# Up weights prepared ahead of the second half's output weights, odd blocks loaded whole, first transposes one block later

## The chip, the core and the metric

The kernel runs on one core of one Trainium2 chip. The metric is device time in microseconds (us), the median of three runs; of one further run there is a hardware profile of every engine. Engines are named as the profile names them: PE is the matrix engine, PEld its weight loads, DVE the vector engine, ACT the scalar engine, POOL is GpSimd, and SP issues the DMAs that are spoken of here.

## The reference, cut to what matters

One hybrid decoder layer over 1024 tokens and 16 meta tokens ahead of them, width 1024:

```python
a = rmsnorm(h, ln_mix_pre[l])
proj = a @ w_in[l]
...
y_diff = diff_attention(dq, dk, dv, ...)
y_hgrn = hgrn2(hq, hf, hi, hg, ...)
mix = jnp.concatenate([y_diff, y_hgrn], axis=-1) @ w_out[l]
h = h + rmsnorm(mix, ln_mix_post[l])
a = rmsnorm(h, ln_ffn_pre[l])
y = conv_ffn(a, w_ffn_up[l], ...)
h = h + rmsnorm(y, ln_ffn_post[l])
```

The change lies where the mixer output is multiplied with `w_out`, normalized, and turned into the transposed input of the up projection.

## The kernel before

**Precision.** Every float32 operand of a product is split into a high and a low part (`split`: an ACT cast makes the high part, a subtraction on DVE or POOL the low one). A product is then three matmuls: high by high, high by low, low by high. `out_part` issues these three for each 128 rows k of `w_out` (L943, L945, L947).

**The stage.** Tokens stand in nine blocks: block 0 is two meta tokens, blocks 1 to 8 are 128 tokens each. `w_out` is used in two halves of 512 output columns. `out_first` does the first half while the last HGRN head (`hgrn_head`) is still being computed: `mix_split` makes high and low parts of the mixer output, hands them to PE in tiles `mm` (four buffers) and stores them to DRAM (`msc`, L932). The k = 7 part depends on the last head and comes last (`out_last`, tiles `pz`). The loop behind it does the second half in the order of blocks 1, 0, 2, 3 ... 8: four pieces c of two k each, read from tiles `mp` that `mix_load` (L950, DMA at L955) brings back from `msc`. There are four `mp` tiles, so piece c of the next block is loaded when PE has read piece c of this one. After a block, `post` loads the residual `xh` (two buffers), normalizes, stores `hsc`, squares on ACT, and makes `a2` on DVE. `trans` (L1061; PE transposes at L1068, ACT copies into `at2`) turns an `a2` round; it stands in the middle of a block's matmuls, ahead of piece 2: `trans(1)` in block 2, `trans(0)` in block 3, `trans(i-2)` in block i. After blocks 1, 2 and 3 two `out_last` each finish the first half of blocks 3 to 8.

**Weights.** `load_wo(n)` (L902) loads eight raw tiles `wor` of `w_out` (tag "wr", three buffers) and splits each into `woh` and `wol` (nine buffers; the second half's k = 3 and later take the slots that the first half's k = 2 and later leave at the end of `out_first`). Odd k are subtracted on DVE, even k on POOL. The up weights are prepared by `prep_plain` (four raw tiles `ra`, split into `uh` and `ul`) and by `prep(q)`, whose sums `ws` (POOL, L1119) also take a "wr" buffer. `ra` has five buffers.

**Order.** PE runs in the order in which the program is written. The orders of ACT, DVE, POOL and SP are made by a scheduler from data dependences, buffers and the order of the program; each engine then works strictly in its own row. All ACT and DVE operations pass through one helper and carry L53. Mixer groups `mix0`, `mix1`, `mix2` are large tiles that are used up one after the other as blocks are split; used-up ones are reused for later tiles.

Of the kernel before, what the change touches and what calls it, by code (L numbers as in the profile page):

```python
# [85 lines left out]
def layer_kernel(ctx: ExitStack, tc: tile.TileContext, x, meta, table, lbl, gpre, gpost, win,  # L86
# [892 lines left out]
    def out_first():  # L979
# [3 lines left out]
        for n, (i, c) in enumerate(todo):  # L983
            if n + 3 < len(todo):
# [12 lines left out]
            if i == NBLK - 1:  # L997
                mix_load(1, c, 0, 2 if c < 3 else 1)
# [11 lines left out]
    close(ma_cm)  # L1010
    wo = load_wo(1)
    close(h_cm, at_p_cm)
# [9 lines left out]
    at2.reverse()  # L1022
    q_cm, qp = pool("p2", 2, "right")
    gpo = qp.tile([P, 512], F32, tag="gpo", name="gpo", bufs=1)
    SY.dma_start(gpo, gpost[:, 512:].to_broadcast([P, 512]))
# [50 lines left out]

    raws, sums, made = {}, {}, {}

    tt = [[None] * 8 for _ in range(2)]
# [29 lines left out]

    def load_raw4(ft):  # L1110
        raws.clear()
        for nm, m, c in (("11", ft, 0), ("22", ft + NF, 1), ("21", ft + NF, 0), ("12", ft, 1)):
            raws[nm] = swp.tile([P, 512], F32, tag="ra", name=f"ra{ft}_{nm}", bufs=5)
            with tc.issue_after(wo0_loaded.ins):
                SY.dma_start(raws[nm], wup[m][:, 512 * c: 512 * (c + 1)])

    def w_sum(nm, a, b, op):
        sums[nm] = wp.tile([P, 512], F32, tag="wr", name=f"ws{nm}", bufs=3)
        G.tensor_tensor(sums[nm], a, b, op=op)  # L1119
        return sums[nm]  # L1120

    def prep(q):
        ft, j = divmod(q, 7)
        if ft >= NF:
            return
        if j == 0:
            load_raw4(ft)
            src = raws["11"]
            w_sum("1", raws["21"], raws["22"], ALU.add)
        elif j == 1:  # L1130
            src = w_sum("2", sums["1"], raws["11"], ALU.subtract)
        elif j == 2:
            src = sums["1"]
        elif j == 3:
            src = w_sum("3", raws["11"], raws["21"], ALU.subtract)
        elif j == 4:
            src = raws["12"]
        elif j == 5:
            src = raws["22"]
        else:  # L1140
            src = w_sum("4", raws["12"], sums["2"], ALU.subtract)
        where = swp if q % 2 else wp
        hi = where.tile([P, 512], F32R, tag="wh", name=f"uh{q}", bufs=4)
        lo = where.tile([P, 512], F32R, tag="wl", name=f"ul{q}", bufs=4)
        split(hi, lo, src, G if j % 2 == 0 and j else V)
        made[q] = (hi, lo)

    plain = {}

    def prep_plain():  # L1150
        load_raw4(0)
        for j, nm in enumerate(("11", "12", "21", "22")):
            where = swp if j % 2 else wp
            hi = where.tile([P, 512], F32R, tag="wh", name=f"uh{nm}", bufs=4)
            lo = where.tile([P, 512], F32R, tag="wl", name=f"ul{nm}", bufs=4)
            split(hi, lo, raws[nm], G)
            plain[nm] = (hi, lo)
# [404 lines left out]
```

## Time and profile before

| quantity | value |
|---|---|
| runs | 1353.58, 1353.48, 1352.76 us; median 1353.48 |
| the profiled execution's own time | 1350.36 us |
| its span, first to last instruction | 1348.6 us |
| mean granted PE clock | 0.995 |
| PE waits of 480 to 800 us | 5.7 + 5.1 + 3.4 + 2.0 + smaller ones |
| DMA share of 640 to 660 us | 0.87 |

A timeline row gives start and duration in us, engine, line, operation, output and inputs by the program's names, shape, and in brackets the idle time ahead of it and what ended it. Consecutive like instructions stand in one row with a count. Matmul starts are exact and their ends modelled, so the distance between starts is the time of one. In a windows row the numbers are the stretch, its length, the busy time of PE, PEld, DVE, ACT and POOL with counts, the granted clock, the DMA share and GB/s. The view of one tile lists its groups as shortest, median and longest duration in ns, with the first and last start.

### The profile page before, as it was taken

The page shows a single profiled execution, that of the slowest core. Times are in us where ns is not written, and L with a number is a line of the kernel's source. Part 1 is how long each engine was busy: PE and PEld are TensorE (multiplying, and loading weights), DVE is VectorE, ACT ScalarE, POOL GpSimd, SP SyncE. Part 2 cuts the span into 40 slices and gives each one's busy share as a digit, 9 for nine tenths or more (in the row PEclk, how much of TensorE's full clock was granted, in tenths as well). Part 3 has the DMA queues.
Part 4 walks back from the last instruction along what each step waited for, and adds up shares of the span by engine and source line. Part 5 has one row for each costly group of instructions (what it writes and reads, how often), then busy time and mean ns, then how long its engine had stood idle before and what let it go on. Part 6 is the DMA issues. An engine that isn't in the chain of part 4 may idle for free.

```text
span 1348.6 us, 26297 instructions
## 1 busy us (share of the span) xinstructions
PE 1293.3 (96%) x10170; PEld 1188.5 (88%) x10170; DVE 929.0 (69%) x1609; ACT 689.9 (51%) x1641; POOL 422.0 (31%) x334
## 2 busy tenths in 40 slices
PE   6999999999999999998898999999999999999997
PEld 5898999989999998676798999999999998888875
DVE  7565657574747474756798787787787776697586
ACT  7465346534654565455574444454444444554453
POOL 3211211021112110234036656656657640010121
PEclk9999999999999999999999999999999999999999
DMA  6331333133211012747712222223221225964253
GB/s 213 107 132 52 103 125 103 44 127 102 103 52 43 22 48 83 232 143 237 243 43 86 95 78 80 79 85 105 79 87 71 79 82 187 336 198 166 87 203 118
DMA packets 84356, 157.01 MB, mean 116 GB/s; under 512 B 9811, under 2 KB 18547, under 8 KB 84230
## 3 DMA queue, kind: packets, MB, share of 16 engines
q1 hardware_dynamic: 84230, 155.33, 34.3%
q8 instruction: 80, 1.31, 0.4%
q14 instruction: 46, 0.38, 0.1%
HBM read 114.66 MB, written 40.63 MB: 115 GB/s over the span
## 4 chain that ended last, share of the span: by engine, by line
PE 59%; DVE 6%; ACT 4%; DMA 4%; issue 3%; POOL 2%; SPq 0%; DVEq 0%; POOLq 0%; ACTq 0%
PE pd L1408 5%; PE pd L1409 5%; PE pd L1407 5%; PE pb L1249 4%; PE pb L1251 4%; PE pb L1250 4%; PE pc L1249 3%; PE pc L1251 2%; PE pc L1250 2%; PE pa L1249 2%; PE pa L1250 2%; PE pa L1251 2%; PE pa L694 1%; PE py L943 1%; PE py L947 1%
## 5 line engine op out<-in xcount | busy, mean ns | idle before, releaser
L1249 PE MATMUL pb<-t,uh 128*128 128x258 f32 x504 | 143.3, 284 | 5.7 <-DVE u L53 5.7
L1251 PE MATMUL pb<-t,ul 128*128 128x258 f32 x504 | 141.7, 281 | 0.0
L1250 PE MATMUL pb<-t,uh 128*128 128x258 f32 x504 | 141.6, 281 | 0.0
L1408 PE MATMUL pd<-wl,gh 128*128 128x512 f32 x308 | 121.9, 396 | 0.1
L1407 PE MATMUL pd<-wh,gh 128*128 128x512 f32 x308 | 121.7, 395 | 0.0
L1409 PE MATMUL pd<-wh,gl 128*128 128x512 f32 x308 | 121.7, 395 | 0.0
L53 DVE SCALAR_TENSOR_TENSOR c<-uu,cwt,c 128x514 f32<-128x514 f32 (+1 forms) x88 | 96.4, 1096 | 20.6 <-ACT c L53 19.9
L1216 POOL TENSOR_TENSOR c<-c,c 128x514 f32<-128x514 f32 (+1 forms) x44 | 63.4, 1440 | 122.8 <-ACT c L53 118.7
L1249 PEld LDWEIGHTS pb<-t,uh 128*128 128x128 f32 x504 | 94.9, 188 | 7.5 <-DVE u L53 6.9
L1251 PEld LDWEIGHTS pb<-t,ul 128*128 128x128 f32 x504 | 95.2, 189 | 0.0
L1250 PEld LDWEIGHTS pb<-t,uh 128*128 128x128 f32 x504 | 95.2, 189 | 0.0
L1250 PE MATMUL pc<-t,uh 128*128 128x258 f32 (+1 forms) x336 | 95.2, 283 | 0.0
L1249 PE MATMUL pc<-t,uh 128*128 128x258 f32 (+1 forms) x336 | 95.0, 283 | 0.0
L1251 PE MATMUL pc<-t,ul 128*128 128x258 f32 (+1 forms) x336 | 95.0, 283 | 0.0
L1249 PE MATMUL pa<-t,uh 128*128 128x258 f32 (+1 forms) x336 | 94.8, 282 | 0.0
L1250 PE MATMUL pa<-t,uh 128*128 128x258 f32 (+1 forms) x336 | 94.5, 281 | 0.0
L1251 PE MATMUL pa<-t,ul 128*128 128x258 f32 (+1 forms) x336 | 94.2, 280 | 0.0
L53 DVE SCALAR_TENSOR_TENSOR c<-ug,cwt,c 128x514 f32<-128x514 f32 (+1 forms) x88 | 86.1, 978 | 2.7 <-ACT c L53 2.0
L145 POOL TENSOR_TENSOR ul<-ws,uh 128x512 fp32r<-128x512 f32 x42 | 59.5, 1416 | 43.8 <-ACT uh L53 39.3
L1408 PEld LDWEIGHTS pd<-wl,gh 128*128 128x128 f32 x308 | 57.7, 187 | 15.1 <-DVE wl L53 0.9
L1409 PEld LDWEIGHTS pd<-wh,gl 128*128 128x128 f32 x308 | 57.7, 187 | 14.0
L1407 PEld LDWEIGHTS pd<-wh,gh 128*128 128x128 f32 x308 | 57.7, 187 | 14.0
(357 smaller groups left out, 4149.5 us busy)
## 6 DMA issues: line engine op xcount, KB each, us to landing
ra<-in_wup_dram SPq DMA_DIRECT2D x88, 256.0 KB, 2.7
wd<-in_wdown_dram SPq DMA_DIRECT2D x44, 256.0 KB, 4.8
tsc<-wd SPq DMA_DIRECT2D x44, 256.0 KB, 3.1
wi<-tsc SPq DMA_DIRECT2D x44, 256.0 KB, 2.8
gi<-gsc SPq DMA_DIRECT2D x33, 256.0 KB, 4.1
wi<-in_wdown_dram SPq DMA_DIRECT2D x33, 256.0 KB, 2.9
mp<-msc SPq DMA_DIRECT2D x31, 256.0 KB, 4.0
msc<-mm SPq DMA_DIRECT2D x24, 256.0 KB, 2.3
```

Source lines behind the costliest of these rows:

```text
L53: ins = call(*args, **kw)
L145: (eng or G).tensor_tensor(lo, raw, hi.bitcast(F32), op=ALU.subtract)
L694: T.matmul(po[:, :P], w_, vn[:, j], start=(j == 0), stop=(j == i))
L943: T.matmul(py[:r], mh, hi, start=(first and k == k0), stop=False)
L947: T.matmul(py[:r], ml, hi, start=False, stop=(last and k == k1 - 1))
L1216: G.tensor_tensor(cg, cg, cu, op=ALU.mult)
L1249: T.matmul(pt, hi[:, s], th[:, k], start=(first and k == 0), stop=False, skip_group_check=True)
L1250: T.matmul(pt, hi[:, s], tl[:, k], start=False, stop=False, skip_group_check=True)
L1251: T.matmul(pt, lo[:, s], th[:, k], start=False, stop=(k == 3), skip_group_check=True)
L1407: T.matmul(py, gh[:, s], wh, start=(k == 0 and pr not in (3, 7)), stop=False, skip_group_check=True)
L1408: T.matmul(py, gh[:, s], wl, start=False, stop=False, skip_group_check=True)
L1409: T.matmul(py, gl[:, s], wh, start=False, stop=(k == NH - 1), skip_group_check=True)
```

## The change

Three things. First, `prep_plain()` and `prep(7)` (with the nine loads of raw up weights) stand ahead of `load_wo(1)`; before, `prep_plain` stood in the last block and `prep(7)` later still. Second, blocks 3, 5 and 7 get one tile for all four pieces, placed in used-up mixer groups; block 3 is loaded after block 1, block 5 after block 3, block 7 after block 5, and even blocks two blocks ahead into the four `mp` tiles. Third, `trans(1)` moves from block 2 to block 3, directly ahead of `trans(0)`; its `a2` goes to a tile of its own.

```diff
     def mix_load(i, c, k0=0, k1=2):
-        if k0 == 0:
+        if i > 1 and i % 2:
+            if c == 0:
+                loaded[i] = mxp.tile([P, 4, 2, 2, P], F32R, tag=f"mix{i // 4}", name=f"mp{i}")
+            loaded[i, c] = loaded[i][:, c]
+        elif k0 == 0:
             loaded[i, c] = mlp.tile([P, 2, 2, P], F32R, tag="mp", name=f"mp{i}_{c}", bufs=4)
...
-    sps = [pair(1, 0), pair(2, 0), pair(1, 1)]
+    sps = [pair(1, 0), pair(2, 0), pair(1, 1), pair(2, 1)]
...
-    wo = load_wo(1)
     close(h_cm, at_p_cm)
...
+    prep_plain()
+    prep(7)
+    wo = load_wo(1)
     gpo = qp.tile([P, 512], F32, tag="gpo", name="gpo", bufs=1)
...
-        if i >= 3 and i % 2:
+        if i == 1:
+            a2 = ep.tile([P, 8, WN[0]], F32, tag="e0", name="a2_1").rearrange("p a c -> p (a c)")[:, :D]
+        elif i >= 3 and i % 2:
...
-        if i == NBLK - 1:
-            prep_plain()
...
-                if i >= 2:
-                    trans((1, 0, 2, 3, 4, 5, 6)[i - 2])
+                if i == 3:
+                    trans(1)
+                    trans(0)
+                if i > 3:
+                    trans(i - 2)
...
-            if i + 1 < NBLK:
-                mix_load(i + 1, c)
+            if i == 1:
+                mix_load(2, c)
+            elif i + 2 < NBLK and i % 2 == 0:
+                mix_load(i + 2, c)
+            elif i > 1 and i + 2 < NBLK and c == 3:
+                for c_ in range(4):
+                    mix_load(i + 2, c_)
+        if i == 1:
+            for c_ in range(4):
+                mix_load(3, c_)
```

`load_raw4`, `w_sum`, `prep` and `prep_plain` are unchanged but for their place, and `prep` now skips a q that is already made.

What this does to the engines' rows is seen at three places. **PE, middle of block 2** (`py1_2`), before the change, with `pa2_1_...` the transposes of block 1:

```order
L945 MATMUL py1_2_7320<-wol1_3_7155,mp2_1_7223 128x512
L947 MATMUL py1_2_7320<-woh1_3_7154,mp2_1_7223 128x512
L1068 MATMUL pa2_1_0_7345<-ident_69,a2_1_7251 128x128 x4
L1068 MATMUL pa2_1_1_7351<-ident_69,a2_1_7251 128x128 x4
L943 MATMUL py1_2_7320<-woh1_4_7160,mp2_2_7239 128x512
L945 MATMUL py1_2_7320<-wol1_4_7161,mp2_2_7239 128x512
```

The same place in block 2 after the change:

```order
L945 MATMUL py1_2_7363<-wol1_3_7215,mp2_1_7261 128x512
L947 MATMUL py1_2_7363<-woh1_3_7214,mp2_1_7261 128x512
L943 MATMUL py1_2_7363<-woh1_4_7220,mp2_2_7277 128x512
L945 MATMUL py1_2_7363<-wol1_4_7221,mp2_2_7277 128x512
```

And the middle of block 3 (`py1_3`) after the change, where only the transposes of block 0 stood before:

```order
L945 MATMUL py1_3_7436<-wol1_3_7215,mp3_7287 128x512
L947 MATMUL py1_3_7436<-woh1_3_7214,mp3_7287 128x512
L1128 MATMUL pa2_1_0_7458<-ident_69,a2_1_7294 128x128 x4
L1128 MATMUL pa2_1_1_7464<-ident_69,a2_1_7294 128x128 x4
L1128 MATMUL pa2_0_0_7470<-ident_69,xh0_7349 128x2 x4
L1128 MATMUL pa2_0_1_7476<-ident_69,xh0_7349 128x2 x4
L943 MATMUL py1_3_7436<-woh1_4_7220,mp3_7287 128x512
L945 MATMUL py1_3_7436<-wol1_4_7221,mp3_7287 128x512
```

The eight transposes of block 1 have left block 2, and stand in block 3 ahead of those of block 0. Nothing else moves on PE.

**ACT and POOL, around the start of block 1's second half.** `jz` are the squares of `out_last` for blocks 0 to 2, `y0` times `gpo0` on POOL the gain that follows them, `ws1` to `ws4` the sums of up weights. ACT before:

```order
L53 COPY y0_6301<-py0_8_7059 128x512
L53 CAST uh9_8080<-ws1_8014 128x512
L53 CAST woh1_6_7172<-wor1_6_7170 128x512
L53 ACTIVATE jz0_7107,ssy_6303<-y0_6301 2x512
L53 ACTIVATE jz1_7120,ssy_6303<-y0_6301 128x512
L53 ACTIVATE ssy_6303<-ssy_6303,eps_74 2x1
L53 ACTIVATE ssy_6303<-ssy_6303,eps_74 128x1
L53 ACTIVATE jz2_7129,ssy_6303<-y0_6301 128x512
L53 CAST woh1_7_7178<-wor1_7_7176 128x512
L53 ACTIVATE ssy_6303<-ssy_6303,eps_74 128x1
L53 CAST mm3_7_7225<-mix1_95 128x128
L53 CAST mm4_7_7229<-mix1_95 128x128
```

ACT after:

```order
L53 CAST woh1_5_7226<-wor1_5_7224 128x512
L53 ACTIVATE jz0_7107,ssy_6303<-y0_6301 2x512
L53 ACTIVATE jz1_7120,ssy_6303<-y0_6301 128x512
L53 ACTIVATE ssy_6303<-ssy_6303,eps_74 2x1
L53 ACTIVATE ssy_6303<-ssy_6303,eps_74 128x1
L53 CAST woh1_6_7232<-wor1_6_7230 128x512
L53 ACTIVATE jz2_7129,ssy_6303<-y0_6301 128x512
L53 CAST mm3_7_7263<-mix1_95 128x128
L53 ACTIVATE ssy_6303<-ssy_6303,eps_74 128x1
L53 CAST mm4_7_7267<-mix1_95 128x128
L53 CAST uh8_8041<-ws2_8039 128x512
L53 CAST woh1_7_7238<-wor1_7_7236 128x512
```

POOL before, in the same stretch:

```order
L145 TENSOR_TENSOR wol1_4_7161<-wor1_4_7158,woh1_4_7160 128x512
L1119 TENSOR_TENSOR ws1_8014<-ra1_21_8010,ra1_22_8008 128x512
L145 TENSOR_TENSOR ul9_8081<-ws1_8014,uh9_8080 128x512
L145 TENSOR_TENSOR wol1_6_7173<-wor1_6_7170,woh1_6_7172 128x512
L1119 TENSOR_TENSOR ws2_8048<-ws1_8014,ra1_11_8006 128x512
L966 TENSOR_TENSOR y0_6301<-y0_6301,gpo0_6304 2x512
L966 TENSOR_TENSOR y0_6301<-y0_6301,gpo0_6304 128x512
L1119 TENSOR_TENSOR ws3_8110<-ra1_11_8006,ra1_21_8010 128x512
L966 TENSOR_TENSOR y0_6301<-y0_6301,gpo0_6304 128x512
L1119 TENSOR_TENSOR ws4_8185<-ra1_12_8012,ws2_8048 128x512
```

POOL after:

```order
L1039 TENSOR_TENSOR ws1_7188<-ra1_21_7184,ra1_22_7182 128x512
L145 TENSOR_TENSOR ul9_8072<-ws1_7188,uh9_8071 128x512
L145 TENSOR_TENSOR wol1_0_7197<-wor1_0_7194,woh1_0_7196 128x512
L145 TENSOR_TENSOR wol1_2_7209<-wor1_2_7206,woh1_2_7208 128x512
L145 TENSOR_TENSOR wol1_4_7221<-wor1_4_7218,woh1_4_7220 128x512
L970 TENSOR_TENSOR y0_6301<-y0_6301,gpo0_6304 2x512
L970 TENSOR_TENSOR y0_6301<-y0_6301,gpo0_6304 128x512
L145 TENSOR_TENSOR wol1_6_7233<-wor1_6_7230,woh1_6_7232 128x512
L1039 TENSOR_TENSOR ws2_8039<-ws1_7188,ra1_11_7180 128x512
L970 TENSOR_TENSOR y0_6301<-y0_6301,gpo0_6304 128x512
```

The casts of `wor1_5`, `wor1_6` and `wor1_7` now stand in this stretch one behind the other with other work between them; on POOL the split of `ws1` has gone ahead of the output weights, and `wol1_6` and the sum `ws2` now stand behind two gains. On ACT `uh8`, which waits for `ws2`, now stands ahead of `woh1_7`. On DVE the subtraction `wol1_7` stands behind `ul8`, the low part of `ws2`. On SP the loads `wor1_5`, `wor1_6` and `wor1_7` are issued only behind all stores of `mm8`; before, only `wor1_6` and `wor1_7` were.

**ACT during the last HGRN head**, while PE does the first half of blocks 3 to 5 between the head's steps. Before:

```order
L53 CAST mm3_6_6535<-mix1_95 128x128
L53 CAST woh1_2_7148<-wor1_2_7146 128x512
L53 CAST mm4_0_6591<-mix1_95 128x256
L53 CAST mm4_2_6601<-mix1_95 128x256
L53 CAST mm4_4_6651<-mix1_95 128x256
L53 COPY y0_6301<-py0_3_6539 128x512
L53 CAST mm4_6_6659<-mix1_95 128x128
L53 CAST mm5_0_6670<-mix1_95 128x256
L53 CAST uh21_7770<-ra0_21_7758 128x512
L53 CAST uh12_7766<-ra0_12_7760 128x512
L53 CAST mm5_2_6720<-mix1_95 128x256
L53 CAST uh22_7774<-ra0_22_7756 128x512
```

After:

```order
L53 CAST mm4_0_6591<-mix1_95 128x256
L53 CAST uh7_7190<-ra1_11_7180 128x512
L53 CAST mm4_2_6601<-mix1_95 128x256
L53 CAST mm4_4_6651<-mix1_95 128x256
L53 CAST uh9_8071<-ws1_7188 128x512
L53 COPY y0_6301<-py0_3_6539 128x512
L53 CAST mm4_6_6659<-mix1_95 128x128
L53 CAST mm5_0_6670<-mix1_95 128x256
L53 CAST woh1_0_7196<-wor1_0_7194 128x512
L53 CAST mm5_2_6720<-mix1_95 128x256
L53 CAST woh1_1_7202<-wor1_1_7200 128x512
L53 CAST mm5_4_6730<-mix1_95 128x256
```

Between the casts of `mm4_4` and `mm4_6` there now stands `uh9`, which waits for the sum `ws1` and so for the loads of raw up weights, and the casts of `wor1_0` and `wor1_1` have come down among those of block 5.

More of the change, by code (lines that the diff above doesn't have):

```diff
@@ L983, in out_first @@
         for n, (i, c) in enumerate(todo):
-            if n + 3 < len(todo):
+            if 0 < n < len(todo) - 3:
                 sps.append(pair(*todo[n + 3]))
@@ L1023, in layer_kernel, with load_raw4, w_sum, prep @@
     q_cm, qp = pool("p2", 2, "right")
+    raws, sums, made = {}, {}, {}
+    def load_raw4(ft):
+        raws.clear()
+        for nm, m, c in (("11", ft, 0), ("22", ft + NF, 1), ("21", ft + NF, 0), ("12", ft, 1)):
+            raws[nm] = swp.tile([P, 512], F32, tag="ra", name=f"ra{ft}_{nm}", bufs=5)
+            with tc.issue_after(wo0_loaded.ins):
+                SY.dma_start(raws[nm], wup[m][:, 512 * c: 512 * (c + 1)])
+    def w_sum(nm, a, b, op):
+        sums[nm] = wp.tile([P, 512], F32, tag="wr", name=f"ws{nm}", bufs=3)
+        G.tensor_tensor(sums[nm], a, b, op=op)
+        return sums[nm]
+    def prep(q):
+        ft, j = divmod(q, 7)
+        if ft >= NF or q in made:
+            return
+        if j == 0:
+            load_raw4(ft)
+            src = raws["11"]
+            w_sum("1", raws["21"], raws["22"], ALU.add)
+        elif j == 1:
+            src = w_sum("2", sums["1"], raws["11"], ALU.subtract)
+        elif j == 2:
+            src = sums["1"]
+        elif j == 3:
+            src = w_sum("3", raws["11"], raws["21"], ALU.subtract)
+        elif j == 4:
+            src = raws["12"]
+        elif j == 5:
+            src = raws["22"]
+        else:
+            src = w_sum("4", raws["12"], sums["2"], ALU.subtract)
+        where = swp if q % 2 else wp
+        hi = where.tile([P, 512], F32R, tag="wh", name=f"uh{q}", bufs=4)
+        lo = where.tile([P, 512], F32R, tag="wl", name=f"ul{q}", bufs=4)
+        split(hi, lo, src, G if j % 2 == 0 and j else V)
+        made[q] = (hi, lo)
+    plain = {}
+    def prep_plain():
+        load_raw4(0)
+        for j, nm in enumerate(("11", "12", "21", "22")):
+            where = swp if j % 2 else wp
+            hi = where.tile([P, 512], F32R, tag="wh", name=f"uh{nm}", bufs=4)
+            lo = where.tile([P, 512], F32R, tag="wl", name=f"ul{nm}", bufs=4)
+            split(hi, lo, raws[nm], G)
+            plain[nm] = (hi, lo)
+    prep_plain()
+    prep(7)
+    wo = load_wo(1)
     gpo = qp.tile([P, 512], F32, tag="gpo", name="gpo", bufs=1)
@@ L1075, in trans @@
                         at2[p][:, ks, lo_ - C0[p]:hi_ - C0[p]], pv[:, :, lo_ - cs.start:hi_ - cs.start])
-    raws, sums, made = {}, {}, {}
     tt = [[None] * 8 for _ in range(2)]
@@ L1108, in t_sums @@
         t_split(p, 5, b21, *last)
[L1110 to L1157, printed above, removed]
     for i in (1, 0, 2, 3, 4, 5, 6, 7, 8):
         py = ps_s(f"py1_{i}")
-        if i == NBLK - 1:
-            prep_plain()
         if i >= 3:
```

## The prediction

> **What bounds the kernel now.** I read the page first, for what the span is made of.
>
> ```profile
> span 1348.6 us, 26297 instructions
> PE 1293.3 (96%) x10170; PEld 1188.5 (88%) x10170; DVE 929.0 (69%) x1609; ACT 689.9 (51%) x1641; POOL 422.0 (31%) x334
> PE 59%; DVE 6%; ACT 4%; DMA 4%; issue 3%; POOL 2%; SPq 0%; DVEq 0%; POOLq 0%; ACTq 0%
> ```
>
> PE is busy 96% of the span and leads the chain that ended last. So the change can gain only where PE stands idle or runs slowly. The windows of 20 us show where that is in the stage that the change touches, and the waits of PE from 480 to 800 us name what ended them.
>
> ```profile
> 600.00:620.00 20.00, 15.30 (x66) 9.29 (x65) 16.12 (x16) 9.52 (x32) 11.58 (x8) 0.96 0.71 229
> 620.00:640.00 20.00, 20.00 (x93) 16.08 (x92) 12.58 (x16) 13.09 (x40) 9.47 (x6) 0.96 0.74 243
> 640.00:660.00 20.00, 17.31 (x87) 13.71 (x86) 12.20 (x15) 11.45 (x35) 0.00 (x0) 1.00 0.87 280
> ```
>
> ```profile
> PE pa L1068 <- DVE a L53: 5.1, 2, 4.4
> PE py L943 <- DMA mp<-msc: 3.4, 2, 2.0
> PE pz L947 <- DVE mm L53: 0.3, 1, 0.3
> ```
>
> PE loses 4.7 us in 600 to 620, and the granted clock (the last column but two) falls to 0.96 there and in the next window; some 2.7 us are lost in 640 to 660, with the DMA engines busy for 0.87. The waits: transposes for `a2`, and `mp` loads.
>
> **The change part by part.** The sum is made against the profiled execution's own 1350.36 us, which is 3.1 below the median of the runs, 1353.48; at the end I put the difference on the median.
>
> *Removed: the stall ahead of trans(1).*
>
> ```profile
> 613.00 0.40 PE L947 MATMUL py<-woh,mp 128*128 128x512 f32 x1
> 617.77 1.42 PE L1068 MATMUL pa<-ident,a 128*128 128x128 f32 x8 [4.38 <-DVE a L53]
> 618.84 0.78 PE L943 MATMUL py<-woh,mp 128*128 128x512 f32 x1
> 621.55 0.48 PE L943 MATMUL py<-woh,mp 128*128 128x512 f32 x1
> 635.01 1.03 PE L1068 MATMUL pa<-ident,a 128*128 128x128 f32 x8
> 635.80 0.48 PE L943 MATMUL py<-woh,mp 128*128 128x512 f32 x1
> ```
>
> From the start at 613.00 to that at 621.55, 8.55 us, PE does the matmul of 613.00, eight transposes and six matmuls. It waits 4.38 us, and the six then take 2.71, 0.45 apiece, where block 1 below takes (602.03 - 597.14) / 21 = 0.233. Without the transposes these seven matmuls take 7 x 0.233 = 1.63. In block 3 the eight transposes take 0.79, as those at 635.01 do, since by then `a2` of block 1 is long made. Saved: 8.55 - 1.63 - 0.79 = **6.1**.
>
> *Removed: the waits for loads and the one for trans(3).*
>
> ```profile
> 642.33 1.09 PE L1068 MATMUL pa<-ident,a 128*128 128x128 f32 x8 [0.69 <-DVE a L53]
> 656.16 0.50 PE L943 MATMUL py<-woh,mp 128*128 128x512 f32 x1 [2.00 <-DMA mp<-msc]
> 662.91 0.47 PE L943 MATMUL py<-woh,mp 128*128 128x512 f32 x1 [1.41 <-DMA mp<-msc]
> ```
>
> Blocks 7 and 8 now have their loads issued a block earlier (7: when block 5 has left the group `mix1`; 8: when block 6 frees the `mp` tiles, a whole block ahead). A block is 24 x 0.233 = 5.6 us, more than the 4.0 that a load takes. So 2.00 + 1.41 go, and with the DVE work of blocks 1 and 2 less crowded also the 0.69: **4.1**. What is late next is a different load, `xh` (below).
>
> *Added: block 1 waits for the last output weights.* Block 1 and what surrounds it before:
>
> ```profile
> 597.14 0.39 PE L943 MATMUL py<-woh,mp 128*128 128x512 f32 x1
> 602.03 0.40 PE L943 MATMUL py<-woh,mp 128*128 128x512 f32 x1
> 602.27 0.40 PE L945 MATMUL py<-wol,mp 128*128 128x512 f32 x1
> 604.56 0.50 PE L947 MATMUL pz<-woh,mm 128*128 128x512 f32 x1 [0.32 <-DVE mm L53]
> ```
>
> ```profile
> 593.48 1.68 SPq L906 DMA_DIRECT2D wor<-in_wout_dram  x2
> 597.79 0.63 ACT L53 ACTIVATE jz<-y 2x512 f32<-2x512 f32 x1
> 600.08 1.29 POOL L1119 TENSOR_TENSOR ws<-ws,ra 128x512 f32<-128x512 f32 x1
> 601.33 3.02 POOL L966 TENSOR_TENSOR y<-y,gpo 2x512 f32<-2x512 f32 x2
> 604.43 3.47 DVE L53 TENSOR_TENSOR ul<-ws,uh 128x512 fp32r<-128x512 f32 x2
> ```
>
> ```profile
> L53 ACT CAST woh<-wor x14: 602/621/625, 530.7 to 600.0; 128x512 fp32r<-128x512 f32 x14
> L53 DVE TENSOR_TENSOR wol<-wor,woh x10: 683/693/1267, 531.3 to 600.6; 128x512 fp32r<-128x512 f32 x10
> L145 POOL TENSOR_TENSOR wol<-wor,woh x4: 1292/1299/1477, 542.5 to 598.7; 128x512 fp32r<-128x512 f32 x4
> DMA to landing us min/median/max: 2.6/3.7/4.1
> ```
>
> The third and fourth parts of `w_out` find their slots free only where the first half ends, as before, so the earliest "wr" buffer is returned at the same place, 593.5. Before, five of the three-buffer rotation's loads were by then through and two were left (the row at 593.48). Now the sum `ws1` holds one of three buffers, and three loads are left. `wor1_5`: issued 593.5, landed 2.6 later at 596.1 (the low end of the row, since nearly nothing else moves there). Then the rows shown in the section on the change, one behind the other: `woh1_5` to 596.7, `jz0` and `jz1` (0.63 each) to 598.0; on POOL the two gains, the first from 597.4, 1.5 apiece, to 600.4; `wol1_6` 1.3, to 601.7; `ws2` 1.29, to 603.0; ACT `uh8` and `woh1_7`, 0.62 each, to 604.2; DVE `ul8` beside them, 1.3 to 1.73 (half of 3.47), to 605.4; `wol1_7` 0.69 to 1.27, to 606.1 or 606.7, and five handovers between engines of some 0.1 to 0.2. PE wants `woh1_7` at 602.03 and `wol1_7` at 602.27. It gets the latter at 606.5 to 607.3: **+4.7**, in two waits with one matmul between them. The 0.32 at 604.56 is swallowed: **-0.3**.
>
> DVE and POOL are at work side by side here, and the row of `wol` on DVE shows what that does: 0.69 as a rule, 1.27 beside POOL's row of 600.08. [...]
>
> *Added: the HGRN phase.* Of the up weights' work, 0.62 on ACT and 1.3 on POOL apiece, most lies in gaps of these engines. But ACT stops at `uh9`. Its `ws1` needs `ra1_21`, whose buffer is returned by the third `ul` on POOL; behind `uh9` stand `mm4_6` and `mm5_0`, which DVE has ahead of a step of the HGRN head, and the casts `woh1_0` and `woh1_1`, whose loads have moved behind the stores of `mm4`.
>
> ```profile
> 557.27 3.99 POOL L145 TENSOR_TENSOR ul<-ra,uh 128x512 fp32r<-128x512 f32 x3 [4.58 <-ACT uh L53]
> 563.01 0.92 PE L430 MATMUL pl<-mix,kr 128*32 128x32 f32 x32 [0.60 <-DVE kr L53]
> 562.07 0.28 DVE L53 TENSOR_TENSOR mix<-mix,tt 128x128 f32<-128x128 f32 x1
> ```
>
> The three `ul` (1.33 each) end at about 550 now, the load lands 3.7 later, sum and cast 1.9: ACT is free at 556, `mm4_6` reaches DVE at 557, its store and then the load of `wor1_1` go at 558, landed 561.6, cast and `wol1_1` to 563, `mm5_4` 0.4: the step of 562.07 starts at 563.3. PE was waiting for this step (0.60), so this goes straight through: +1.2. Below: the moved subtraction `ul7` has left this very place, and a load of 2.6 would make it 0. [...] I take **+1.0**.
>
> *Added: a limit at trans(6).*
>
> ```profile
> xh<-in_x_dram SPq DMA_DIRECT2D x8, 512.0 KB, 4.8
> 647.78 0.74 DVE L53 SCALAR_TENSOR_TENSOR xh<-y,ssy,xh 128x512 f32<-128x512 f32 x1
> 651.65 1.28 DVE L53 SCALAR_TENSOR_TENSOR a<-xh,ssy,gfb 128x1024 f32<-128x1024 f32 x1 [2.46 <-ACT ssy L53]
> ```
>
> SP now has the load of block 6's `xh` behind block 8's four `mp` loads, which wait until PE has read block 6. Before, the start at 656.16 is that of block 7's seventh matmul: ahead of it lie the wait of 2.00, the first six (1.40) and a modelled tail of 0.16, so block 6 ends at 652.6. With the terms that come ahead of it (-6.1 + 0.4, -0.7, -0.3, +4.7, +1.0) that is 651.6 now. The `xh` load goes out behind the last `mp` load, at 652.0, and lands 4.8 later; from `xh` to the end of `a2`, 651.65 - 647.78 + 1.28 = 5.15, it is 662.0. PE came to trans(6) 12 x 0.233 after 662.91 and a tail, at 665.8; it comes 1.0 and 3.4 earlier, at 661.4: **+0.6** (nothing with a load of 4 us, 1.5 with one of 5.7). Two sets of transposes in a row in block 3 want two PSUM banks back from ACT, whose squares `jz` stand ahead: **+0.4**, at most the 1.2 of two squares.
>
> *The sum.* -6.1 - 4.1 - 0.3 + 4.7 + 1.0 + 0.6 + 0.4 = **-3.8**: 1346.6 against the execution's own 1350.36, and **1349.7** on the median of 1353.48. The dense DVE work behind 665 starts earlier by the same amount and keeps the gain.
>
> **The rivals.**
>
> *The wait in block 1 is short.* If ACT takes `woh1_6` and `woh1_7` as soon as they land and the gains on POOL start with `jz0` rather than behind `woh1_5`, 2 us of the 4.7 remain. For it: the two gains are of 1.5 us because DVE worked beside them, and one alone could take 1.3. Against: the row is a chain of ten, and each engine keeps to its row. It gives -3.8 - 2.7 = -6.5, 1347.0.
>
> *The two waits in block 1 cool PE.* The 4.38 above was followed by six matmuls of 0.45 apiece and a granted clock of 0.96, while a wait of 2.00 was not:
>
> ```profile
> 533.56 0.50 PE L943 MATMUL py<-woh,mm 128*128 128x512 f32 x1 [2.00 <-DVE gate L53]
> ```
>
> (the next starts 0.33 later, and then 0.24). If the two waits count as one, up to six matmuls run 0.2 slower: +1.2, -2.6 in all, 1350.9. [...]
>
> [...]
>
> *The change doesn't do what it says*: loads of odd blocks stay behind waiting ones on SP, and what the stall gives back comes again at trans(2) or trans(4): +3.8, about 1353.5.
>
> **How the numbers follow.** Forecast 0.45, short wait 0.16, cooling 0.12, no effect 0.07, HGRN phase 0.20. About 0.2%, 2.7 us, is what a measurement of this kernel can tell from no change: faster means below 1350.8. My forecast lies just beyond that, so of its 0.45 some 0.32 count as faster and 0.13 as the same; with the short wait faster is 0.48, same 0.13 + 0.12 + 0.07 = 0.32, slower 0.20. The range reaches from the short wait with no loss in the HGRN phase (-7.5) and a little below to near the HGRN rival's end: 1345.5 to 1357.0.
>
> **What would show it.** In the new profile: no wait at the transposes of block 1, and one set of 16 transposes in block 3; PE waiting at the k = 7 matmuls of block 1 for `woh` and `wol`, 2 to 2.5 us each; no `mp` wait in blocks 7 and 8; a wait of up to 1.5 us on `a` at trans(6); POOL's `ul` rows ahead of 552, and block 1's start at 598 rather than 597.1. A start of block 1 beyond 600 would show the HGRN rival; a wait at block 1 below 2 or above 7 us would make my largest added term wrong.

## The result, and the profile after

The changed kernel takes 1354.39 us, the median of 20 runs, beside 1352.51 of 20 runs of the kernel before: a ratio of 1.0013, 95% interval 0.9999 to 1.0026. That is within 0.2%. One of the 20 runs before took 2531.25 us and is not among those of the ratio. The forecast was 1349.7 (-0.28% of the 1353.48 of three runs); the measured time lies inside the stated range, but the gain did not come. The range held because it was wide enough to take in the rivals, not because the sum was right. The two profiled executions have the same span, so what follows is a shift inside it.

The page and the waits of PE from 480 to 800 us, after the change:

```profile
span 1348.6 us, 26282 instructions
```

```profile
PE pl L436 <- DVE mix L53: 4.1, 2, 2.5
PE pa L1128 <- DVE a L53: 2.8, 2, 2.6
PE py L943 <- ACT woh L53: 1.9, 1, 1.9
```

The 4.4 us ahead of `trans(1)` and the waits for `mp` are gone. In their place stand two waits for the last output weights, a wait for `a2` at `trans(6)`, and more waiting in the HGRN head. The windows show a second loss, which no row of waits shows:

```profile
600.00:620.00 20.00, 16.59 (x60) 9.64 (x59) 13.84 (x16) 8.92 (x27) 11.38 (x9) 0.83 0.66 209
620.00:640.00 20.00, 19.68 (x99) 16.04 (x98) 13.56 (x17) 14.17 (x45) 6.70 (x5) 1.00 0.84 277
640.00:660.00 20.00, 19.74 (x99) 16.18 (x98) 13.05 (x13) 12.49 (x32) 2.59 (x2) 1.00 0.81 271
```

From 620 to 660 PE is all but full, as forecast. In 600 to 620 it is busy 16.59 us with 60 matmuls, where 66 took 15.30 before: the granted clock is 0.83. PE's row in the timeline shows where:

```profile
598.85 0.39 PE L943 MATMUL py<-woh,mp 128*128 128x512 f32 x1
...
603.60 0.40 PE L947 MATMUL py<-woh,mp 128*128 128x512 f32 x1
605.91 0.78 PE L943 MATMUL py<-woh,mp 128*128 128x512 f32 x1 [1.91 <-ACT woh L53]
608.19 0.79 PE L945 MATMUL py<-wol,mp 128*128 128x512 f32 x1 [1.49 <-DVE wol L53]
...
609.21 0.63 PE L943 MATMUL pz<-woh,mm 128*128 128x512 f32 x1
...
612.62 0.48 PE L947 MATMUL py<-woh,m 128*2 128x512 f32 x1
612.93 0.40 PE L943 MATMUL py<-woh,m 128*2 128x512 f32 x1
...
617.77 0.40 PE L943 MATMUL py<-woh,mp 128*128 128x512 f32 x1
...
624.77 0.39 PE L943 MATMUL py<-woh,mp 128*128 128x512 f32 x1
...
629.60 0.50 PE L943 MATMUL py<-woh,mp 128*128 128x512 f32 x1
...
665.57 1.06 PE L1128 MATMUL pa<-ident,a 128*128 128x128 f32 x8 [2.57 <-DVE a L53]
```

Block 1 starts at 598.85, block 2 at 617.77, block 3 at 624.77. From 609.21 to 612.62 eight matmuls stand (612.62 - 609.21) / 8 = 0.426 us apart, not 0.233.

The same matmuls in both profiles give the account, each step counted from the one ahead of it:

| stretch of PE's row | before, us | after, us | difference | forecast |
|---|---|---|---|---|
| wait for `gate` to the last `ss` (end of the HGRN head) | 56.34 | 59.22 | +2.88 | +1.0 |
| `ss` to the start of block 2 | 20.53 | 26.15 | +5.62 | +4.4 |
| block 2 | 14.01 | 7.00 | -7.01 | -6.9 |
| block 3 to behind its transposes | 3.48 | 4.83 | +1.35 | +1.2 |
| to behind `trans(5)` | 30.54 | 27.59 | -2.95 | -2.7 |
| to behind `trans(6)` | 8.12 | 9.20 | +1.08 | -0.8 |
| sum | | | +0.97 | -3.8 |

(The forecast's terms are split by place: -6.1 is -6.9 in block 2 and +0.8 for the transposes in block 3, and the 1.41 of the load waits belongs to the last row.) The wait for `gate` before is the 533.56 in the prediction. The other three rows of PE that bound the head are the `ss` before,

```profile
589.90 0.55 PE L554 MATMUL ss<-ident,on 128*128 128x128 f32 x3 [0.26 <-DVE on L53]
```

and the wait for `gate` and the `ss` after:

```profile
532.40 0.50 PE L943 MATMUL py<-woh,mm 128*128 128x512 f32 x1 [2.00 <-DVE gate L53]
591.62 0.55 PE L554 MATMUL ss<-ident,on 128*128 128x128 f32 x3 [0.26 <-DVE on L53]
```

The gains are there as forecast. Three costs are larger: the HGRN head by 1.9, block 1 by 1.2, `trans(6)` by 1.9. The stretches of the table together are 0.97 us longer although the spans are equal, since the profile after reaches the wait for `gate` 1.16 us earlier (532.40 beside 533.56). So this pair of profiles hides about 1 us of loss, and the medians of the runs, 1.9 us apart, show it.

### The profile page after: what moved, and what is told of

Read it like the earlier page. It is cut to its first block, busy times and chain, and to the rows that moved or that the text cites. A ratio compares the mean times of both kernels' runs of the same rounds, so it can differ in the third digit from the quotient of the medians.

```text
span 1348.6 us, 26282 instructions
## 1 busy us (share of the span) xinstructions
PE 1293.8 (96%) x10170; PEld 1189.0 (88%) x10170; DVE 930.3 (69%) x1609; ACT 690.8 (51%) x1641; POOL 423.7 (31%) x334
## 3 DMA queue, kind: packets, MB, share of 16 engines
q8 instruction: 80, 1.31, 0.4%
## 4 chain that ended last, share of the span: by engine, by line
PE 68%; DVE 7%; ACT 4%; issue 3%; DMA 3%; POOL 2%; SPq 0%; DVEq 0%; ACTq 0%; POOLq 0%
PE pd L1426 5%; PE pd L1427 5%; PE pd L1425 5%; PE pb L1267 4%; PE pb L1269 4%; PE pb L1268 4%; PE pc L1267 3%; PE pc L1269 3%; PE pc L1268 3%; PE pa L1267 2%; PE pa L1268 2%; PE pa L1269 2%; PE pa L694 2%; PE py L943 1%; PE py L945 1%
```

## The experiments

All ratios are to the kernel before, with 95% intervals. Three numbers of each profile go with them: the HGRN head (`gate` to `ss`), block 1's start to block 2's start, and `ss` to the first matmul of the up projection (`pq`). A profile is of one execution, so these numbers need not follow the ratio; that of trans_only is of the slowest of its twelve runs (1356.39, where their median is 1351.01).

| kernel | preparation | ratio | HGRN head, us | block 1 to 2, us | `ss` to `pq`, us |
|---|---|---|---|---|---|
| before | late | 1 | 56.34 | 13.29 | 79.55 |
| after | ahead | 1.0013 [0.9999, 1.0026] | 59.22 | 18.92 | 77.64 |
| no_prep_ahead | late | 0.9975 [0.9962, 0.9989] | 57.19 | 13.28 | 74.59 |
| prep_ahead_only | ahead | 1.0023 [1.0008, 1.0038] | 58.08 | 18.99 | 81.37 |
| trans_only | late | 0.9980 [0.9966, 0.9994] | 62.90 | 13.32 | 77.10 |
| loads_only | late | 0.9994 [0.9979, 1.0009] | 57.74 | 13.29 | 80.20 |
| sum_elsewhere | ahead | 0.9999 [0.9986, 1.0012] | 60.14 | 12.66 | 76.80 |
| sum_behind | half ahead | 0.9988 [0.9977, 1.0000] | 60.38 | 13.36 | 76.90 |
| pz_first | ahead | 1.0010 [0.9997, 1.0024] | 61.67 | 15.50 | 75.24 |
| xh_early_apart | late | 0.9951 [0.9936, 0.9967] | 57.39 | 13.33 | 72.16 |
| xh_early_only | ahead | 0.9986 [0.9972, 1.0001] | 61.29 | 18.13 | 75.36 |
| apart_wider | late | 0.9967 [0.9954, 0.9981] | 57.67 | 13.30 | 73.33 |
| all_mended | ahead | 0.9973 [0.9962, 0.9984] | 60.66 | 12.64 | 73.17 |

The first four experiments take the change apart. The theory: the preparation ahead costs what the other two parts gain, by holding a "wr" buffer in block 1 (and the HGRN head). The rival: the loads or the transposes bring the new waits.

### no_prep_ahead: the change without its first part

```diff
+    wo = load_wo(1)
     close(h_cm, at_p_cm)
-    prep_plain()
-    prep(7)
-    wo = load_wo(1)
...
+        if i == NBLK - 1:
+            prep_plain()
```

> The change without its first part: loads and transposes as in the changed kernel, the preparation of up weights at its old place. Theory (the parts add up: the preparation ahead costs 2.9 us in the HGRN phase and 5.6 at block 1, the rest gains): the changed kernel's +1.3 less 8.5, so 7 us faster than before, 1346, with no waits on woh or wol in block 1 and the wait at trans(6) of 2.6 kept. Rival (the gains need the preparation ahead, because otherwise the sums and splits of up weights crowd DVE and POOL at 600 to 613 and a2 of block 1 or 2 is late again): 0 to 3 us faster, with new waits at trans(2) or trans(3).

It is the faster kernel, by 0.25% (1349.73 us), with both waits of block 1 gone: the first part of the change is what costs. But it gains 3.4 us, about half of what was expected. PE's row in block 3 shows where the rest went:

```profile
622.70 1.03 PE L1126 MATMUL pa<-ident,a 128*128 128x128 f32 x8
625.40 0.89 PE L1126 MATMUL pa<-ident,xh 2*128 2x2 f32 x8 [1.67 <-ACT at L53]
...
627.64 0.63 PE L947 MATMUL py<-woh,mp 128*128 128x512 f32 x1
```

ACT, in the same stretch, copies the first transposes only behind two squares:

```profile
622.88 0.63 ACT L53 ACTIVATE jz<-y 128x512 f32<-128x512 f32 x1 [1.15 <-DVE y L53]
...
623.84 0.61 ACT L53 ACTIVATE jz<-y 128x512 f32<-128x512 f32 x1
...
624.78 1.23 ACT L53 COPY at<-pa 128x512 f32<-128x512 f32 x3
```

PE comes to the transposes earlier than in the changed kernel, relative to what ACT does, so the second set waits 1.67 us for the two PSUM banks. Eight matmuls behind it stand 0.43 apart (627.25 to 630.63), which costs another 3.38 - 8 x 0.233 = 1.5. At `trans(6)` it waits 2.06. In the changed kernel the waits of block 1 held PE back and hid this: that the 0.4 of the forecast came out there was luck.

### prep_ahead_only: the first part alone

The loads and the transposes are as before; `prep_plain` and `prep(7)` stand ahead of `load_wo(1)`.

```diff
+    prep_plain()
+    prep(7)
+    wo = load_wo(1)
...
-        if i == NBLK - 1:
-            prep_plain()
```

> Only the first part: preparation ahead of the second half's output weights, loads and transposes as before. Theory: 2.9 us lost in the HGRN phase and 5.6 at block 1, less what the stall at trans(1) loses by having its DVE and POOL work out of the way (at most 4.4): 4 to 8.5 us slower, 1357 to 1361. Rival (the 2.9 and 5.6 of the changed kernel come from loads of block 3 or from the later transposes): no slower than 2 us.

Slower by 0.23%, or 3.1 us, where 4 to 8.5 were expected; it is the only one whose interval lies wholly above 1. Block 1's waits are there in full (1.93 and 1.59, and 18.99 us to block 2). A row of PE shows something that the forecast did not have:

```profile
622.05 1.06 PE L1122 MATMUL pa<-ident,a 128*128 128x128 f32 x8 [1.53 <-DVE a L53]
```

With `trans(1)` left in block 2, its stall falls from 4.38 to 1.53. Of these 2.85 us, 1.9 are an `a2` that is ready 13.1 and not 15.0 us behind the end of block 1, and 0.9 are the slow matmuls behind block 1, which bring PE there later. So part of what the move of the transposes gains, the preparation ahead gains too: the two parts do not add up. That `a2` is earlier because sums and splits of up weights have left DVE and POOL there is likely, but no run isolates it.

### trans_only and loads_only: the third and the second part alone

```diff
-                if i >= 2:
-                    trans((1, 0, 2, 3, 4, 5, 6)[i - 2])
+                if i == 3:
+                    trans(1)
+                    trans(0)
+                if i > 3:
+                    trans(i - 2)
```

> Only the third part: transposes of block 1 moved to block 3, everything else as before. Theory: the stall goes, 7.0 less 1.35 for the two sets of transposes in block 3, and the load waits of blocks 7 and 8 (3.4) stay: 5.7 faster, 1347. Rival (the stall only moves to trans(2) or trans(3) as long as the up weights' work stands at 600 to 613): 0 to 2 faster.

Faster by 0.20%, 2.7 us, about half of what was expected. PE's waits from 590 to 690 us:

```profile
PE py L943 <- ACT py L53: 1.9, 1, 1.9
PE py L943 <- DMA mp<-msc: 1.9, 2, 1.0
```

The stall is gone, and 1.9 us of it come again at the start of block 3, where `py1_3` wants the PSUM bank into which ACT still writes the squares of block 0. Behind this wait seven matmuls of block 3 stand 0.43 apart (627.85 to 630.83), another 1.3 us.

loads_only is the kernel before with the tiles and `mix_load` calls of the change:

```diff
+        if i > 1 and i % 2:
+            if c == 0:
+                loaded[i] = mxp.tile([P, 4, 2, 2, P], F32R, tag=f"mix{i // 4}", name=f"mp{i}")
```

> Only the second part: odd blocks whole, even blocks two ahead. Theory: the load waits of blocks 7 and 8 go (3.4), and a wait of up to 2.5 at trans(6) for the load of xh behind the loads of block 8 comes: 1 to 3.4 faster. Rival (the loads are hidden by the transposes' waits anyway): within 1 us.

No difference (0.9994). The waits for `mp` are gone and stand at the next place, `a2`:

```profile
PE pa L1072 <- DVE a L53: 7.2, 3, 4.1
```

That is 4.06 at `trans(1)`, 0.63 and 2.5 at `trans(6)`; the last one is new, and xh_early_only below traces it, in the changed kernel, to the load of `xh`. Each part alone gains less than its own removed waits: trans_only meets ACT's squares next, and loads_only the load that it has itself put late.

### sum_elsewhere and sum_behind: is it the "wr" buffer?

The sum `ws1` of `prep(7)` goes to a tile "e1" that is free then, so `load_wo(1)` has all three "wr" buffers:

```diff
+        if first:
+            sums[nm] = ep.tile([P, 8, WN[0]], F32, tag="e1", name=f"ws{nm}").rearrange("p a c -> p (a c)")[:, :512]
+        else:
             sums[nm] = wp.tile([P, 512], F32, tag="wr", name=f"ws{nm}", bufs=3)
```

> The changed kernel with one edit: the first sum of the preparation ahead (ws1 of prep(7)) lies in an unused tile of its own and no longer in one of the three wr buffers. Theory (the sum's hold on a buffer is what makes block 1 wait): wor1_5 is loaded early again, the 1.9 and 1.5 us waits on woh and wol in block 1 and the slow matmuls behind them go, about 5 us less than the changed kernel, 1349 to 1350 where before is 1353; the HGRN phase stays as it is in the changed kernel. Rival (ACT and POOL rows are simply too full there): the waits stay above 2 us and the time within 1.5 of the changed kernel's.

Block 1 to block 2 takes 12.66 us, 6.26 less than in the changed kernel: both waits and the slow matmuls go. SP's rows, of the changed kernel and of this one, show the buffer: two loads of `wor` are left to the end of the first half, and not three.

```profile
595.21 4.70 SPq L906 DMA_DIRECT2D wor<-in_wout_dram  x3
```

```profile
596.90 1.67 SPq L906 DMA_DIRECT2D wor<-in_wout_dram  x2
```

So the held buffer is the cause of the waits. But from `ss` to `pq` only 0.84 us are left of the gain, and the time, 0.9999, lies only 1.9 us below the changed kernel's, where 5 were expected. PE's waits from 590 to 690 us:

```profile
PE pa L1131 <- DVE a L53: 3.3, 2, 2.7
PE py L943 <- ACT py L53: 1.7, 1, 1.7
```

1.66 us return at block 3's start, 1.67 between the two sets of transposes, and 1.7 at `trans(6)`: the wait there is hardly longer than in the changed kernel (2.68 beside 2.57), but six slow matmuls follow it here and none there. The wait between the transposes is, by contrast, followed by no slow matmul, where the same wait of no_prep_ahead was followed by eight:

```profile
627.59 0.89 PE L1131 MATMUL pa<-ident,xh 2*128 2x2 f32 x8 [1.67 <-ACT at L53]
```

```profile
620.00:636.00 16.00, 12.59 (x65) 9.97 (x64) 12.83 (x16) 11.25 (x36) 4.49 (x4) 1.00 0.90 295
```

The granted clock of this stretch is 1.00; in no_prep_ahead it is 0.91 from 620 to 640. The squares of block 0, written into the bank that block 3 wants, in ACT's row:

```profile
620.83 1.02 ACT L53 ACTIVATE py<-xh 2x1024 f32<-2x1024 f32 x1 [0.39 <-DVE xh L53]
```

With the accumulator read behind them (621.79, 0.18) they end at 621.97, and PE starts at 622.03.

sum_behind puts only `prep(7)` behind `load_wo(1)`:

```diff
     prep_plain()
-    prep(7)
     wo = load_wo(1)
+    prep(7)
```

> The changed kernel with prep(7) back behind the second half's output weights, the four plain up weights still ahead. Theory: as with the sum elsewhere, no waits on woh or wol in block 1; and since the casts of the first output weights stand in the HGRN phase where they stood before, nothing is lost there either: 4 to 6 us less than the changed kernel, 1348 to 1350. If the HGRN phase costs what I forecast (1 us) it is about 1 us faster than the sum elsewhere; if that phase's 2.9 in the profile was chance, both are alike.

Again block 1 is free (13.36 us), and 1.68 between the transposes and 2.59 at `trans(6)` follow. 0.9988, with an interval that ends at 1; 4 to 6 us less than the changed kernel were expected, and 3.4 came. It is 1.5 us faster than sum_elsewhere, but the intervals overlap, so this comparison does not settle what the HGRN head costs.

### pz_first: the waits of block 1 kept, but with work between them

The two `out_last` behind block 1 go ahead of its last piece, so PE has six more matmuls before it wants the late weights.

```diff
+            if i == 1 and c == 3:
+                for p in (3, 4):
+                    for _ in out_last(p):
+                        pass
...
-        if i < 4:
+        if 1 < i < 4:
```

> The changed kernel with the six matmuls of out_last for blocks 3 and 4 moved ahead of the last piece of block 1, so that PE has 1.4 us of work where it waits. Theory (PE cools because its two waits in block 1 add up to 3.4 us with one matmul between): the waits shrink to about 2.0, the ten matmuls at 0.43 go, 1.4 + 2 = 3.4 less than the changed kernel. Rival (the slow matmuls have another cause): 1.4 less, and the slow matmuls stay.

Block 1 to block 2 takes 3.42 us less than in the changed kernel. PE's row there:

```profile
610.57 0.50 PE L943 MATMUL py<-woh,mp 128*128 128x512 f32 x1 [0.64 <-ACT woh L53]
612.85 0.50 PE L945 MATMUL py<-wol,mp 128*128 128x512 f32 x1 [1.78 <-DVE wol L53]
...
613.42 0.39 PE L943 MATMUL py<-woh,m 128*2 128x512 f32 x1
```

```profile
600.00:620.00 20.00, 17.57 (x74) 10.38 (x73) 12.11 (x15) 10.38 (x32) 13.51 (x10) 1.00 0.56 185
```

The first wait is 0.64 in place of 1.91, the second as long as it was (2.28 from start to start in both), and not one matmul is slow: the granted clock is 1.00 where it was 0.83. So the second wait did not bring them by itself here. Of the kernels that keep both waits whole, all three have slow matmuls behind them: 11 in the changed kernel and in prep_ahead_only, 7 in xh_early_only. The run's time (1.0010) does not show the gain; the HGRN head took 61.67 in this profile, of which more below.

### xh_early_only and xh_early_apart: the wait at trans(6)

The residual `xh` of blocks 4 and later is loaded at the block's start, ahead of the block's `mp` loads on SP, and not in `post`. In xh_early_only this alone is added to the changed kernel; xh_early_apart is no_prep_ahead with this, and with `trans(1)` one piece ahead of `trans(0)`.

```diff
+            if c == 0 and i >= 4:
+                xhs[i] = xh_load(i)
             if c == 2:
...
                 if i == 3:
-                    trans(1)
                     trans(0)
...
+            if c == 1 and i == 3:
+                trans(1)
```

> The changed kernel with one edit: the residual xh of blocks 4 to 8 loaded at the start of the block, ahead of the next loads of mixer output. Theory: the 2.6 us wait at trans(6) goes and PE comes to the plain units 2.5 earlier; part may come back there, since DVE is nearly full behind 670: 1 to 2.5 less than the changed kernel, 1352 where before is 1353. Rival (a2 of block 6 is late for other reasons): the wait stays and the time is that of the changed kernel.

The wait of 2.57 at `trans(6)` goes, and from `ss` to `pq` 77.64 becomes 75.36. Of these 2.3 us, 0.8 lie in block 1, ahead of the edit, where fewer matmuls are slow; from block 2's start to `pq` it is 1.5. The ratio of 0.9986 stands beside 1.0013 of the changed kernel: their intervals overlap in little. SP's row and DVE's:

```profile
658.54 0.37 SPq L1093 DMA_DIRECT2D xh<-in_x_dram  x1
```

```profile
662.98 0.75 DVE L53 SCALAR_TENSOR_TENSOR xh<-y,ssy,xh 128x512 f32<-128x512 f32 x1 [0.55 <-DMA xh<-in_x_dram]
```

The load of block 6's `xh` leaves SP at 658.54, 1.4 us ahead of the block's end and ahead of block 8's `mp` loads, and DVE has it 3.0 us behind that end. In the changed kernel it leaves at 654.85, 1.2 us behind the block's end and behind four `mp` loads, lands 5.4 later, and DVE has it 6.7 us behind that end.

> The loads and the later transposes without the preparation ahead, and two more edits: the residual xh of blocks 4 to 8 is loaded at the start of the block, so ahead of the mixer loads, and the transposes of block 1 stand one piece ahead of those of block 0. Theory: the wait of 2.1 at trans(6) goes, and the 1.7 between the two sets of transposes with the eight slow matmuls behind it (1.6): about 5 less than without these edits, 8 less than before, 1345. Rival (trans(6) is late for ACT and DVE work and not for the load, and the two sets wait for their a2): within 1.5 of the kernel without these edits.

The fastest kernel of the study: 0.9951, 1346.39 us (median of six runs). That is 6.6 us less than before, where 8 were expected, and 3.2 less than no_prep_ahead, where 5 were. What is left of waits from 590 to 690 us:

```profile
PE pq L1258 <- ACT ug L53: 1.6, 1, 1.6
PE pa L1133 <- ACT at L53: 1.6, 2, 1.3
```

The 1.3 is at the transposes of block 0, and seven matmuls behind it still stand 0.43 apart (627.60 to 630.58).

### apart_wider and all_mended: the rest

apart_wider moves `trans(0)` one more piece back (c = 3), away from `trans(1)`; all_mended does the same with the preparation ahead and `ws1` in "e1". Both have the early `xh`.

```diff
+            if i == 3 and c in (1, 3):
+                trans(c // 2 ^ 1)
```

> The fastest so far (no preparation ahead, xh early) with the transposes of block 0 moved one more piece back, to the last piece of block 3. Theory (the second set waits for ACT, whose copies stand behind the squares of out_last, and the wait cools PE): the 1.3 wait and the 1.6 of slow matmuls go, 2 to 3 less, 1344, ratio 0.993. Rival (ACT is late by more than a piece): the wait only gets shorter, within 1 of the fastest so far.

> The changed kernel with its preparation ahead kept and all three mends: the first sum in a tile of its own, xh early, the two sets of transposes two pieces apart. Theory (what the sum elsewhere gave back was lost to the two sets of transposes and trans(6)): now the 6.3 of block 1 come through: 5 to 8 less than the changed kernel, 1347; beside the same without preparation ahead it shows what that costs in the HGRN phase, 1 to 3 us. Rival (the preparation ahead pays once it is unhindered): faster than the same without it.

Neither beats xh_early_apart (0.9967, 0.9973), and apart_wider misses the 0.993 that was expected of it; all_mended comes 5.4 us below the changed kernel, within the 5 to 8 expected. In apart_wider the wait at `trans(0)` falls to 0.26 and no matmul behind it is slow, but PE now comes to `trans(4)` too early:

```profile
648.17 1.10 PE L1133 MATMUL pa<-ident,a 128*128 128x128 f32 x8 [2.67 <-DVE a L53]
```

PE is 2.9 us earlier in this profile than in that of xh_early_apart, and DVE with this `a2` only 0.3. One microsecond of the difference is this step, which now falls beside a sum on POOL:

```profile
641.61 1.75 DVE L53 SCALAR_TENSOR_TENSOR xh<-y,ssy,xh 128x512 f32<-128x512 f32 x1
```

```profile
641.52 1.29 POOL L1040 TENSOR_TENSOR ws<-ra,ra 128x512 f32<-128x512 f32 x1 [5.30 <-DMA mp<-msc]
```

The step takes 0.74 in xh_early_apart, where it starts at 642.92 and POOL's sum at 643.20, behind it; the step after it stands beside POOL in both and takes 1.8 in both. From `ss` to `pq` all_mended and apart_wider are alike (73.17 and 73.33), and their ratios' intervals overlap, so even without its waits the preparation ahead shows no gain.

## Why the prediction was off

**The stall ahead of trans(1), the load waits, the two sets of transposes.** Right in the changed kernel: -7.01, +1.35 and -2.95 beside -6.9, +1.2 and -2.7. The wait of 0.24 between the transpose sets is even below the 0.4. But the forecast took these terms for properties of the edits, and the experiments show that they hang on when PE arrives: without block 1's waits 1.67 to 1.68 appear between the two sets (no_prep_ahead, sum_elsewhere, sum_behind).

**Block 1's wait for the last output weights.** The mechanism was right and shown by sum_elsewhere. The chain in the changed kernel, ACT's row and DVE's:

```profile
604.72 0.62 ACT L53 CAST uh<-ws 128x512 fp32r<-128x512 f32 x1 [2.93 <-POOL ws L1039]
605.25 0.61 ACT L53 CAST woh<-wor 128x512 fp32r<-128x512 f32 x1
```

```profile
605.37 1.09 DVE L53 TENSOR_TENSOR ul<-ws,uh 128x512 fp32r<-128x512 f32 x1 [1.81 <-ACT uh L53]
606.38 1.75 DVE L53 TENSOR_TENSOR wol<-wor,woh 128x512 fp32r<-128x512 f32 x1
```

`uh8` holds ACT for 2.93 us ahead of the last cast, and `wol1_7` takes 1.75 beside POOL's sum of 605.88 (1.71), where the `wol` on DVE at 598.87 took 0.68. The delay itself is (605.91 - 603.60 - 0.23) + (608.19 - 605.91 - 0.23) = 4.1, a little under the 4.7. **The step that failed here is the one on the clock**: the forecast put slow matmuls behind these two waits at nothing in its sum, and as a rival (cooling) at a chance of 0.12 and 1.2 us, on the ground that none had followed a single wait of 2.00. They came, and cost more: from 608.19 to 612.93 there are 11 matmuls, 4.74 - 11 x 0.233 = 2.2 us. With block 1's 0.63 that it swallows (13.29 before, 12.66 in sum_elsewhere, against the 0.3 of the forecast) this makes 4.1 + 2.2 - 0.6 = 5.7, beside 5.63 measured from block 1's start to block 2's.

That the waits bring the slow matmuls is shown: the three kernels with both waits whole have them in block 1 (7 or 11, mostly 0.43 apart), and those without these waits have none there (block 1 to block 2 in 12.6 to 13.4 us). How many follow, and after how long a wait, is not fixed. In xh_early_only 7 follow the same two waits, at 1.4 us. At one place, between the two sets of transposes, a wait of 1.67 or 1.68 is followed by eight slow matmuls in no_prep_ahead, by seven in sum_behind, and by none in sum_elsewhere. Single waits of 1.93 (trans_only) and 1.31 (xh_early_apart) are followed by seven, and of 2.57 (the changed kernel, `trans(6)`) and 2.67 (apart_wider, `trans(4)`) by none. So the ground of the forecast, one wait without slow matmuls behind it, could not carry the step, and pz_first, a single profile, does not prove that both waits are needed. What decides whether a wait is followed by slow matmuls is not shown by any run here.

**trans(6).** Forecast 0.6 with an upper end of 1.5; measured 2.57. The mechanism (the `xh` load behind the `mp` loads on SP) is shown by xh_early_only, the size was off. DVE's row and SP's:

```profile
660.39 0.75 DVE L53 SCALAR_TENSOR_TENSOR xh<-y,ssy,xh 128x512 f32<-128x512 f32 x1 [1.93 <-DMA xh<-in_x_dram]
...
664.14 1.28 DVE L53 SCALAR_TENSOR_TENSOR a<-xh,ssy,gfb 128x1024 f32<-128x1024 f32 x1
```

```profile
652.69 1.73 SPq L959 DMA_DIRECT2D mp<-msc  x3
654.85 1.17 SPq L1091 DMA_DIRECT2D xh<-in_x_dram  x2
```

From `xh` to the end of `a2` it is 5.03, as forecast (5.15). But block 6 ends at 653.67 and the load goes out at 654.85, 1.2 later and not 0.4, with four `mp` loads ahead of it still under way (issued from 652.26 on, 4.1 to 4.5 to landing), and lands after 5.4 and not 4.8. That is 1.4 of the 2.0 that are missing; another 0.5 is PE, which came to `trans(6)` 9.3 us behind block 6's end and not 9.8.

**The HGRN head.** Forecast +1.0, in this pair of profiles +2.88. Its mechanism can be seen: `uh9` waits for the sum on POOL and holds ACT, DVE waits for a cast behind it, and the step that PE waits for comes late. ACT's row, then PE's:

```profile
556.32 0.62 ACT L53 CAST uh<-ws 128x512 fp32r<-128x512 f32 x1 [5.10 <-POOL ws L1039]
```

```profile
550.71 1.01 PE L436 MATMUL pl<-mix,kr 128*32 128x16 f32 x63 [2.48 <-DVE mix L53]
...
561.40 0.75 PE L436 MATMUL pl<-mix,kr 128*32 128x16 f32 x64 [1.62 <-DVE mix L53]
```

The 1.62 is this hold, met one step of the head earlier than forecast; the kernel before has no wait there, and its 0.60 at the next step is gone. The 2.48 ahead of it was not forecast, and stands where the kernel before waits 1.07.

The other profiles tell the two apart, since PE does the same matmuls in the same order over the head in every kernel. The first 300 of them hold the 2.48, the next 250 the 1.62:

| part of the head | six with late preparation, us | sum_behind, us | six with the preparation ahead, us |
|---|---|---|---|
| first 300 matmuls | 17.3 to 19.8, median 18.3 | 20.9 | 18.7 to 20.0, median 19.4 |
| next 250 | 17.7 to 18.0, one 21.8 (trans_only), median 17.9 | 18.1 | 17.7 to 20.7, median 19.6 |
| the rest | 21.3 | 21.3 | 21.3 |

In all six kernels with the whole preparation ahead ACT stands idle for 3.8 to 6.7 us at `uh9`; in the others `uh9` does not stand in the head. So the hold costs about 1.7 us, an estimate from the medians of the second row, where 1.0 was forecast. The 1.1 of the first row lies ahead of `uh9` and is not the hold's; whether it belongs to the change is not settled.

For the whole head the kernels with late preparation, whose orders are the same up to here, take 56.34 to 62.90 us, median 57.5, and the six others 58.08 to 61.67, median 60.4: a difference of 2.9 against a spread of 6.6 within one order. Another way to it: what a kernel's time has moved, its ratio less 1 times 1352.9, less what its stretch from `ss` to `pq` has moved from 79.55, leaves what lies outside that stretch. For the six with the preparation ahead the median is +2.7 (1.3 to 5.7), for the five others with late preparation +0.8 (-1.5 to +1.8). So some 2 to 3 us for the whole head are probable, as an estimate from these medians, above the 1.0 of the forecast. The upper end of the range, 1357.0, and the 0.20 for the HGRN phase stood on a larger cost of the preparation there, an estimate that no run shows; in its place the runs showed these 2 to 3 us, and block 1 started at 598.85, short of the 600 that was to show it.

**The sum.** By the rows of the account, what the change adds came to 2.9 + 5.6 + 0.5 + 2.5 = 11.5 (HGRN head, block 1, the two sets of transposes, `trans(6)`) where 6.4 was forecast; what it removes came to 10.6, with 10.2 forecast. The rival of slow matmuls behind the two waits came true, and two terms that were too small on top of it, the HGRN head and `trans(6)`, took the gain away. All of this is the account of one pair of profiles; the size of the slow stretch and of the head differs between executions.

## What to carry to other kernels

A buffer lent to early preparation is paid for by the last load of the pool that it came from: count the buffers at the place where PE wants the last tile. A wait that is removed ahead of a chain on other engines mostly moves to the next place where PE meets that chain (sum_elsewhere freed 6.3 us and kept 0.8; 1.7 of what came again were mostly slow matmuls), so add up removed waits only as far as the next meeting point. And look for the load that a moved load has been put ahead of: issuing `xh` earlier took the wait of 2.57 at `trans(6)` and 1.5 us of the stretch from block 2 to `pq` off the changed kernel. Here a single wait of 1.31 to 2.68 us on PE was followed by some seven slow matmuls, about 1.4 us, or by none; one profile in which none followed does not rule them out.

## What the runs showed that was not expected

- The same wait at the same place, 1.67 us between two sets of transposes, was followed by eight matmuls at 0.43 in place of 0.233 in one kernel (no_prep_ahead) and by none in another (sum_elsewhere). In xh_early_apart a wait of 1.31 was enough.
- The same instructions in the same order took 56.34 to 62.90 us over the HGRN head in six single profiles, so a single profile cannot price a change there to better than some microseconds.
